# Moving operands shifted by spare bytes, so that each TensorE product reads at a chosen offset from its weights

## The chip, the cores and the metric

One NeuronCore of a Trainium2 chip runs the program. The metric is device time in microseconds (us), from the first to the last instruction of the program and what the runtime puts around it; lower is better.

## The reference

Two layers on a sequence of 256 tokens with 2048 features, in float32:

```python
h = x
h = h + conv_pool_mixer(rms_norm(h))   # w_in 2048x3072, 31-tap conv + layer norm, pools, w_out 2048x2048
h = h + swiglu(rms_norm(h))            # w_gate, w_up 2048x5632, w_down 5632x2048
h = h + short_conv_mixer(rms_norm(h))  # w_in 2048x6144, 3-tap conv, w_out 2048x2048
h = h + swiglu(rms_norm(h))
return rms_norm(h)
```

Nearly all the arithmetic is matrix products of the 256 tokens with weights, which are read once each from HBM (some 390 MB).

## The kernel before, in words

Activations lie with features on the 128 partitions and tokens along the free dimension. The weights come as 5904 blocks of 128x128, in the order in which they are used, in DMA units of at most 16 blocks (tile `w`). ScalarE rounds eight blocks at a time to float32r (`hi`, L114), VectorE or sometimes GpSimd subtracts to get the rest (`lo`, L121). Each `hi` and `lo` tile has 4096 bytes in a partition, a block 512.

An activation chunk of 128 features is split in the same way: its high half lies in the first 256 columns of a slice, its low half in the next 256 (2048 bytes together). These moving operands are four tiles: `xs` (16 slices, filled by each norm), `cat` (8 slices, the halves of the first mixer's output), `y` (22 slices, half of a SwiGLU's hidden layer) and `z` (16 slices, the short convolution's output).

For each block `product` issues one of two forms. The **wide** form, in both SwiGLUs and the second mixer, is one matmul of `hi` with all 512 columns (L163) and one of `lo` with the first 256 (L164): two weight loads and 768 columns. The **narrow** form, in the first mixer and for the last chunk of the last SwiGLU, is three matmuls of 256 columns (L166 and L167 with `hi`, L168 with `lo`): three weight loads and 768 columns.

All of a block's operands start at a multiple of 512 bytes from the start of their tiles, and the weight tiles have a multiple of 256. So within one stage the distance from the start of the weights to the start of the moving operand, modulo 256 bytes, is one number, which this document calls the **offset**. By the addresses in the built program it is 0 for `xs`, 32 for `cat`, and 96 for `y` and `z`.

A program-wide order of the instructions is set at build time; the pieces `hi` and `lo` are prepared four ahead of their use (LOOK), the DMAs one unit further. The first mixer's convolution runs on VectorE and ScalarE beside the products.

Of the kernel before, what the change touches and what calls it, by code (L numbers as in the profile page):

```python
# [12 lines left out]
F32R = mybir.dt.float32r  # L13
# [4 lines left out]
P = 128  # L18
T = 256
D = 2048  # L20
NC = D // P
DC = 1024
NA = DC // P
FF = 5632
NF = FF // P
NH = NF // 2
# [46 lines left out]
WARM = 9  # L73

KEEP = 8

POOL_SPLIT = range(96, 24 * NC + 16 + 7 * NC + 8)

# [6 lines left out]
def block_kernel(ctx: ExitStack, tc: tile.TileContext, xT: bass.AP, xtok: bass.AP, vec: bass.AP, wall: bass.AP, out: bass.AP):  # L85
    nc = tc.nc
    const = ctx.enter_context(tc.tile_pool(name="const", bufs=1))
    act = ctx.enter_context(tc.tile_pool(name="act", bufs=1))
# [35 lines left out]
    def next_block():  # L124
        b, i = cursor
        at = UNIT_AT[PIECES[i][0]] + PIECES[i][1]
        if b == at + PIECES[i][2]:
            ready.pop(i)
            i, at = i + 1, b
        for j in range(i, i + LOOK + 1):  # L130
            prepare(j)
        if i + LOOK < len(PIECES):
            for u in range(PIECES[i + LOOK][0] + 1, PIECES[i + LOOK][0] + AHEAD + 1):
                fetch(u)
        cursor[:] = [b + 1, i]
        hi, lo = ready[i]
        o = (b - at) * P
        return hi[:, o : o + P], lo[:, o : o + P]
# [8 lines left out]
    def tick():  # L147
        for name, q in queues.items():
            credit[name] = credit[name] + 1.0 if q else 0.0
            while q and credit[name] >= PACE[q[0][0]]:  # L150
                cost, step = q.popleft()
                credit[name] -= PACE[cost]
                step()

    def drain():
        while any(queues.values()):
            for q in queues.values():
                if q:
                    q.popleft()[1]()

    def product(acc, hi, lo, x, first, last, wide):
        if wide:
            nc.tensor.matmul(acc, hi, x, start=first, stop=False, skip_group_check=True)  # L163
            nc.tensor.matmul(acc[:, T:], lo, x[:, :T], start=False, stop=last, skip_group_check=True)  # L164
        else:
            nc.tensor.matmul(acc[:, :T], hi, x[:, :T], start=first, stop=False)  # L166
            nc.tensor.matmul(acc[:, :T], hi, x[:, T:], start=False, stop=False)  # L167
            nc.tensor.matmul(acc[:, :T], lo, x[:, :T], start=False, stop=last)  # L168

    def matmul_chunks(xs, ks, n=1, wide=False, behind=None):  # L170


        accs = [ps.tile([P, 2 * T], F32, name="acc") for _ in range(n)]
        for i, k in enumerate(ks):
            first, last = i == 0, i == len(ks) - 1
            for acc in accs:
                hi, lo = next_block()
                product(acc, hi, lo, xs[:, k, :], first, last, wide)
                tick()
            if behind is not None:  # L180
                behind(k)
        return accs
# [10 lines left out]
    def split(dst, src, scale=None):  # L193

        if scale is None:
            nc.scalar.copy(dst[:, :T], src)
            nc.vector.tensor_tensor(out=dst[:, T:], in0=src, in1=dst[:, :T], op=ALU.subtract)
        else:
            nc.scalar.activation(dst[:, :T], src, AF.Copy, scale=scale)
            nc.vector.scalar_tensor_tensor(out=dst[:, T:], in0=src, scalar=scale, in1=dst[:, :T], op0=ALU.mult, op1=ALU.subtract)  # L200
# [4 lines left out]
    def col(name, i):  # L205
        return v[:, VECS[name] + i : VECS[name] + i + 1]

    identity = v[:, VECS["identity"] :]
    h = act.tile([P, NC, T], F32, name="h")
    xs = act.tile([P, NC, 2 * T], F32R, name="xs")  # L210
    ones = const.tile([P, P], F32, name="ones")
    nc.gpsimd.memset(ones, 1.0)

# [14 lines left out]
    def rsqrt_of(*totals, scale, halves=False, st=None):  # L228
# [9 lines left out]
        if halves:  # L238

            idle = ps.tile([P, P], F32, name="idle", tag="acc")  # L240
            with tc.issue_after(mm.ins):
                for _ in range(KEEP):
                    nc.tensor.matmul(idle, ones, ones, start=True, stop=True)  # L243
# [27 lines left out]
    class Norm:  # L271


        def __init__(self, gain, final=False):
            self.gain, self.final = gain, final
            self.sums = []

        def add(self, c):
# [6 lines left out]

        def scale(self, c):
            if not self.final:
                split(xs[:, c, :], h[:, c, :], col(self.gain, c))

        def square(self, c):  # L290
            if c == 0:
# [16 lines left out]
    def project(src, ks, norm=None, wide=False, narrow_end=False):  # L308

        for n in range(NC):  # L310
            if narrow_end and n == NC - 1:
                wide = False
            (acc,) = matmul_chunks(src, ks, wide=wide)
            if wide:
                t = phase[0].tile([P, T], F32, name="cross", bufs=3)
                nc.scalar.copy(t, acc[:, T:])
                nc.vector.tensor_tensor(out=h[:, n, :], in0=h[:, n, :], in1=t, op=ALU.add)
            nc.vector.tensor_tensor(out=h[:, n, :], in0=acc[:, :T], in1=h[:, n, :], op=ALU.add)  # L318
            if norm is not None:
                norm.add(n)  # L320

    def scaled(acc, r, name, wide=False):
        if not wide:
            s = (phase[0] if name == "pv" else tmp).tile([P, T], F32, name=name, bufs=2)
            nc.vector.tensor_tensor(out=s, in0=acc[:, :T], in1=r, op=ALU.mult)
            return s
        s = summed(acc, name)
        nc.vector.tensor_tensor(out=s, in0=s, in1=r, op=ALU.mult)
        return s


    norm = Norm("mix_norm_e")
    nc.sync.dma_start(v[:, :NC], vec[:, :NC])

    def load(at, n):
# [30 lines left out]
    every = range(NC)  # L366
    with tc.tile_pool(name="m0", bufs=1) as m0, tc.tile_pool(name="ps_side", bufs=2, space=PSUM) as ps_side:
# [1 line left out]
        a_in = m0.tile([P, NA, pad + T], F32, name="a_in")  # L369
        nc.gpsimd.memset(a_in[:, :, :pad], 0.0)  # L370
        conv = m0.tile([P, NA, T], F32, name="conv")
        cat = m0.tile([P, NA, 2 * T], F32R, name="cat")
        total = m0.tile([P, 2, T], F32, name="total")

        sides, prods, state = {}, {}, {}
# [156 lines left out]

        project(xs, POOL_CHUNKS)
        drain()
        norm = Norm("ffn_norm0")
        project(cat, range(NA), norm)

    def swiglu(norm, following):
        with tc.tile_pool(name="ffn", bufs=1) as fp:
            phase[0] = fp  # L540
            y = fp.tile([P, NH, 2 * T], F32R, name="y")
            r = None
            for half in range(2):
                for f in range(NH):
                    (acc_g,) = matmul_chunks(xs, every, wide=True)
                    (acc_u,) = matmul_chunks(xs, every, wide=True)
                    if r is None:
                        r = norm.rstd()
                    gate = scaled(acc_g, r, "gate", True)
                    up = scaled(acc_u, r, "val", True)  # L550
                    nc.scalar.activation(gate, gate, AF.Silu)
                    nc.vector.tensor_tensor(out=up, in0=up, in1=gate, op=ALU.mult)
                    split(y[:, f, :], up)
                project(y, range(NH), following if half else None, wide=True, narrow_end=half and following.final)
# [1 line left out]
    x0.close()  # L556


    after = Norm("mix_norm_o")
    swiglu(norm, after)  # L560


    norm = Norm("ffn_norm1")
    with tc.tile_pool(name="m1", bufs=1) as m1:
        phase[0] = m1
        z = m1.tile([P, NC, 2 * T], F32R, name="z")
        pad = SW - 1
        r = None
        for c in range(NC):
            (acc_c,) = matmul_chunks(xs, every, wide=True)  # L570
            (acc_v,) = matmul_chunks(xs, every, wide=True)
            if r is None:
                r = after.rstd()
            cg = scaled(acc_c, r, "gate", True)
            vv = scaled(acc_v, r, "val", True)
            cv = m1.tile([P, pad + T], F32, name="cv", bufs=2)
            nc.gpsimd.memset(cv[:, :pad], 0.0)
            nc.vector.tensor_tensor(out=cv[:, pad:], in0=cg, in1=vv, op=ALU.mult)
            wc = VECS["conv_w_o"] + c * SW
            co = m1.tile([P, T], F32, name="co", bufs=2)  # L580
            nc.vector.tensor_scalar(out=co, in0=cv[:, :T], scalar1=v[:, wc : wc + 1], scalar2=None, op0=ALU.mult)
            for k in range(1, SW):
                nc.vector.scalar_tensor_tensor(out=co, in0=cv[:, k : k + T], scalar=v[:, wc + k : wc + k + 1], in1=co, op0=ALU.mult, op1=ALU.add)
            (acc_b,) = matmul_chunks(xs, every, wide=True)
            bg = scaled(acc_b, r, "pv", True)
            nc.vector.tensor_tensor(out=bg, in0=bg, in1=co, op=ALU.mult)
            split(z[:, c, :], bg)
        project(z, every, norm, wide=True)


    last = Norm("final_norm", final=True)
    swiglu(norm, last)
    halves = rsqrt_of(*last.sums, scale=1.0 / D, halves=True)
    with tc.tile_pool(name="fin", bufs=1) as fin:

# [90 lines left out]
```

## Time and profile before

| | |
|---|---|
| three runs | 2104.46, 2105.78, 2109.65 us; median 2105.78 |
| profiled execution | 2103.73 us, of which the span of the trace is 2102.0 |
| TensorE matmul busy | 2079.1 us (99%), 12584 records |
| weight loads busy | 1855.8 us (88%), beside the matmuls |
| VectorE, ScalarE, GpSimd busy | 66%, 50%, 10% |
| weights' DMA queue | 393.52 MB, 52.4% of 16 engines' time |
| TensorE's granted clock | 0.997 of full speed, mean |

A matmul's duration in the profile is from its start to its modelled end, and successive matmuls overlap; how fast they follow each other is read from the distance between their starts.

### The profile page before, as it was taken

What the parts mean: (1) busy time and instruction counts of PE and PEld (TensorE: products, weight loads), DVE (VectorE), ACT (ScalarE), POOL (GpSimd) and SP (SyncE); (2) the same over time, 40 slices, a digit from 0 to 9 for tenths busy, and PEclk for the clock granted to TensorE, in tenths of its full rate; (3) what the DMA queues carried; (4) which work ended last, traced back from release to release, by engine and by line L of the source; (5) the groups of instructions that cost most, each with busy time, mean ns of one, the idle gap of its engine ahead of it and who ended that gap; (6) DMA issues with size and microseconds to landing.
All of it is one profiled execution on the core that took longest, in us unless ns stands there. A gap on an engine that the chain in (4) does not pass through costs nothing.

```text
span 2102.0 us, 31608 instructions
## 1 busy us (share of the span) xinstructions
PE 2079.1 (99%) x12584; PEld 1855.8 (88%) x12584; DVE 1383.4 (66%) x1979; ACT 1060.9 (50%) x1571; POOL 200.6 (10%) x180
## 2 busy tenths in 40 slices
PE   8999999999999999999999999999999999999998
PEld 8999988888888888888888888888888888888887
DVE  6888866666556666666777777666666556666654
ACT  7776654444444444454444445554444444444453
POOL 3985200000000000011000001100000000000011
PEclk9999999999999999999999999999999999999999
DMA  8554455555555555555555555555555555555551
GB/s 326 187 191 168 158 184 197 183 198 182 194 185 188 193 187 194 183 196 182 183 198 182 198 183 193 180 189 198 183 196 184 189 192 183 198 182 199 182 192 68
DMA packets 56884, 395.53 MB, mean 188 GB/s; under 512 B 6432, under 2 KB 7200, under 8 KB 9760
## 3 DMA queue, kind: packets, MB, share of 16 engines
q1 hardware_dynamic: 56736, 393.52, 52.4%
q8 instruction: 98, 1.61, 0.3%
q14 instruction: 50, 0.41, 0.1%
HBM read 391.39 MB, written 2.10 MB: 187 GB/s over the span
## 4 chain that ended last, share of the span: by engine, by line
PE 98%; DMA 1%; DVE 1%; ACT 0%; SPq 0%; issue 0%; DVEq 0%; ACTq 0%
PE acc L163 57%; PE acc L164 30%; PE acc L166 4%; PE acc L168 4%; PE acc L167 4%; DMA rows<-in_xtok 0%; DMA h<-in_xT 0%; DVE res L603 0%; ACT hi L114 0%; PE st L237 0%; PE st L268 0%; DVE lo L121 0%; SPq L104 0%; ACT conv L475 0%; PE idle L243 0%
## 5 line engine op out<-in xcount | busy, mean ns | idle before, releaser
L114 ACT CAST hi<-w 128x1024 fp32r<-128x1024 f32 (+1 forms) x740 | 776.1, 1050 | 975.3 <-PE acc L163 621.0
L121 DVE TENSOR_TENSOR lo<-w,hi 128x1024 fp32r<-128x1024 f32 (+1 forms) x691 | 845.2, 1224 | 639.5 <-ACT hi L114 635.3
L163 PE MATMUL acc<-xs,hi 128*128 128x512 f32 x3584 | 1243.3, 391 | 0.0
L164 PE MATMUL acc<-xs,lo 128*128 128x256 f32 x3584 | 1004.7, 280 | 0.0
L163 PEld LDWEIGHTS acc<-xs,hi 128*128 128x128 f32 x3584 | 670.4, 187 | 146.2
L164 PEld LDWEIGHTS acc<-xs,lo 128*128 128x128 f32 x3584 | 678.1, 189 | 0.1
L163 PE MATMUL acc<-y,hi 128*128 128x512 f32 x1386 | 485.2, 393 | 0.0
L164 PE MATMUL acc<-y,lo 128*128 128x256 f32 x1386 | 386.4, 279 | 0.0
L163 PEld LDWEIGHTS acc<-y,hi 128*128 128x128 f32 x1386 | 259.4, 187 | 61.7
L164 PEld LDWEIGHTS acc<-y,lo 128*128 128x128 f32 x1386 | 259.9, 187 | 0.4
L298 POOL TENSOR_TENSOR sumsq<-sumsq,sq 128x256 f32<-128x256 f32 x56 | 58.8, 1050 | 1599.1 <-ACT sq L296 1599.1
L166 PE MATMUL acc<-xs,hi 128*128 128x256 f32 x512 | 144.0, 284 | 5.2 <-ACT hi L114 4.2
L167 PE MATMUL acc<-xs,hi 128*128 128x256 f32 x512 | 143.6, 283 | 0.0
L168 PE MATMUL acc<-xs,lo 128*128 128x256 f32 x512 | 141.3, 284 | 0.1
L121 POOL TENSOR_TENSOR lo<-w,hi 128x1024 fp32r<-128x1024 f32 x49 | 118.7, 2441 | 43.1 <-PE acc L167 34.3
L166 PEld LDWEIGHTS acc<-xs,hi 128*128 128x128 f32 x512 | 98.1, 192 | 6.2 <-ACT hi L114 5.0
L167 PEld LDWEIGHTS acc<-xs,hi 128*128 128x128 f32 x512 | 98.2, 192 | 0.0
L168 PEld LDWEIGHTS acc<-xs,lo 128*128 128x128 f32 x512 | 96.5, 192 | 0.5 <-DVE lo L121 0.5
L163 PE MATMUL acc<-z,hi 128*128 128x512 f32 x256 | 89.6, 393 | 0.0
L188 ACT COPY cross<-acc 128x256 f32<-128x256 f32 x224 | 80.6, 360 | 0.0
L164 PE MATMUL acc<-z,lo 128*128 128x256 f32 x256 | 71.3, 279 | 0.0
L318 DVE TENSOR_TENSOR h<-acc,h 128x256 f32<-128x256 f32 x112 | 47.2, 423 | 18.9 <-PE acc L168 13.2
(134 smaller groups left out, 1198.6 us busy)
## 6 DMA issues: line engine op xcount, KB each, us to landing
w<-in_wall SPq DMA_DIRECT2D x365, 1024.0 KB, 4.8
w<-in_wall SPq DMA_DIRECT2D x7, 512.0 KB, 7.7
rows<-in_xtok SPq DMA_DIRECT2D x2, 1024.0 KB, 7.9
h<-in_xT SPq DMA_DIRECT2D x7, 256.0 KB, 7.3
out<-res SPq DMA_DIRECT2D x2, 512.0 KB, 2.8
out<-res SPq DMA_DIRECT2D x2, 384.0 KB, 2.8
v<-in_vec SPq DMA_DIRECT2D x1, 260.0 KB, 6.7
h<-in_xT SPq DMA_DIRECT2D x2, 128.0 KB, 2.3
```

Of the source, the lines that this page charges most:

```text
L114: nc.scalar.copy(hi[:, : n * P], w)
L121: engine.tensor_tensor(out=lo[:, : n * P], in0=w, in1=hi[:, : n * P], op=ALU.subtract)
L163: nc.tensor.matmul(acc, hi, x, start=first, stop=False, skip_group_check=True)
L164: nc.tensor.matmul(acc[:, T:], lo, x[:, :T], start=False, stop=last, skip_group_check=True)
L166: nc.tensor.matmul(acc[:, :T], hi, x[:, :T], start=first, stop=False)
L167: nc.tensor.matmul(acc[:, :T], hi, x[:, T:], start=False, stop=False)
L168: nc.tensor.matmul(acc[:, :T], lo, x[:, :T], start=False, stop=last)
L188: nc.scalar.copy(t, acc[:, T:])
L298: nc.gpsimd.tensor_tensor(out=self.sums[0], in0=self.sums[0], in1=sq, op=ALU.add)
L318: nc.vector.tensor_tensor(out=h[:, n, :], in0=acc[:, :T], in1=h[:, n, :], op=ALU.add)
```

## The change

Each moving tile gets some spare bytes (`xs` 256, the others 128), and the operands become views that start some bytes into the tile. `xs` is now used at two places: 32 bytes in for the first mixer, 160 bytes in for the other three norms. `y` and `z` start 64 bytes in. `cat` starts where it did. Who reads and writes what, the number of instructions and their order on every engine stay as they are.

```diff
+XS_M0 = 32
+XS_F0 = 160
+XS_M1 = 160
+XS_F1 = 160
+Y_F0 = 64
+Y_F1 = 64
+Z_M1 = 64
+CAT = 0
...
-    xs = act.tile([P, NC, 2 * T], F32R, name="xs")
+    xs_room = act.tile([P, NC * 2 * T + 64], F32R, name="xs")
+    def moving(room, at, n):
+        return room[:, at // 4 : at // 4 + n * 2 * T].rearrange("p (c t) -> p c t", c=n)
...
-        def __init__(self, gain, final=False):
+        def __init__(self, gain, at=0, final=False):
             self.gain, self.final = gain, final
+            self.xs = moving(xs_room, at, NC)
...
-                split(xs[:, c, :], h[:, c, :], col(self.gain, c))
+                split(self.xs[:, c, :], h[:, c, :], col(self.gain, c))
...
-        cat = m0.tile([P, NA, 2 * T], F32R, name="cat")
+        cat = moving(m0.tile([P, NA * 2 * T + 32], F32R, name="cat"), CAT, NA)
...
-            y = fp.tile([P, NH, 2 * T], F32R, name="y")
+            y = moving(fp.tile([P, NH * 2 * T + 32], F32R, name="y"), at, NH)
...
-                    (acc_g,) = matmul_chunks(xs, every, wide=True)
-                    (acc_u,) = matmul_chunks(xs, every, wide=True)
+                    (acc_g,) = matmul_chunks(norm.xs, every, wide=True)
+                    (acc_u,) = matmul_chunks(norm.xs, every, wide=True)
...
-        z = m1.tile([P, NC, 2 * T], F32R, name="z")
+        z = moving(m1.tile([P, NC * 2 * T + 32], F32R, name="z"), Z_M1, NC)
```

The weight tiles move up by 256 bytes, which leaves the offsets as the numbers say:

| products | blocks | offset before | offset now |
|---|---|---|---|
| wide, `xs` | 3584 | 0 | 160 |
| wide, `y` and `z` | 1386 + 256 | 96 | 160 |
| narrow, `xs` | 512 | 0 | 32 |
| narrow, `cat` | 144 | 32 | 32 |
| narrow, `y` (last chunk) | 22 | 96 | 160 |

## Rows read from the trace of the kernel before

**Rows 1.** The page: the span, busy time by engine, and the slices' granted clock.

```profile
span 2102.0 us, 31608 instructions
...
PE 2079.1 (99%) x12584; PEld 1855.8 (88%) x12584; DVE 1383.4 (66%) x1979; ACT 1060.9 (50%) x1571; POOL 200.6 (10%) x180
...
PEclk9999999999999999999999999999999999999999
```

**Rows 2.** What TensorE's instructions waited for: us in total, times, longest.

```profile
PE acc L166 <- ACT hi L114: 4.2, 3, 1.7
PE acc L166 <- ACT cat L477: 3.4, 1, 3.4
PE st L268 <- DVE diag L260: 2.8, 1, 2.8
```

**Rows 3.** By stage: us, busy us (records) of each engine, clock, DMA.

```profile
core 0: us, PE busy (x) PEld busy (x) DVE busy (x) ACT busy (x) POOL busy (x), PEclk, DMA share, GB/s
0.00:47.00 47.00, 40.77 (x310) 39.25 (x311) 27.95 (x52) 34.30 (x53) 10.61 (x40) 1.00 0.89 342
47.00:260.00 213.00, 205.82 (x1703) 204.64 (x1702) 183.04 (x324) 153.98 (x266) 142.27 (x83) 0.98 0.50 178
260.00:505.00 245.00, 245.00 (x1417) 216.23 (x1417) 158.69 (x227) 120.49 (x179) 0.00 (x0) 1.00 0.53 188
```

**Rows 4.** Wide hi matmuls in stretches of xs, y, z: count, durations, first and last start.

```profile
L163 PE MATMUL acc<-xs,hi x616: 390/391/392, 290.6 to 503.8; 128*128 128x512 f32 x154
L163 PE MATMUL acc<-y,hi x321: 392/394/395, 515.8 to 627.8; 128*128 128x512 f32 x161
L163 PE MATMUL acc<-z,hi x224: 392/393/394, 1273.9 to 1352.0; 128*128 128x512 f32 x112
```

**Rows 5.** The same for narrow first matmuls: xs twice, cat, y.

```profile
L166 PE MATMUL acc<-xs,hi x136: 283/283/284, 55.0 to 103.6; 128*128 128x256 f32 x136
...
L166 PE MATMUL acc<-xs,hi x87: 283/283/284, 165.0 to 196.0; 128*128 128x256 f32 x87
...
L166 PE MATMUL acc<-cat,hi x93: 277/280/281, 226.9 to 259.1; 128*128 128x256 f32 x93
...
L166 PE MATMUL acc<-y,hi x22: 279/282/285, 2080.9 to 2088.5; 128*128 128x256 f32 x22
```

**Rows 6.** Timeline of a wide stretch: start us, duration us.

```profile
300.01 0.39 PE L163 MATMUL acc<-xs,hi 128*128 128x512 f32 x1
300.24 0.28 PE L164 MATMUL acc<-xs,lo 128*128 128x256 f32 x1
300.35 0.39 PE L163 MATMUL acc<-xs,hi 128*128 128x512 f32 x1
```

**Rows 7.** Counts of the products by moving tile, whole span, and of the start.

```profile
L163 PE MATMUL acc<-xs,hi 128*128 128x512 f32 x3584 | 1243.3, 391 | 0.0
...
L163 PE MATMUL acc<-y,hi 128*128 128x512 f32 x1386 | 485.2, 393 | 0.0
...
L163 PE MATMUL acc<-z,hi 128*128 128x512 f32 x256 | 89.6, 393 | 0.0
...
L166 PE MATMUL acc<-cat,hi x144: 277/280/583, 150.4 to 259.1; 128*128 128x256 f32 x144
...
L166 PE MATMUL acc<-xs,hi x97: 278/283/385, 4.7 to 46.8; 128*128 128x256 f32 x97
```

**Rows 8.** Preparation of weights: busy us, mean ns of one, idle before.

```profile
L121 DVE TENSOR_TENSOR lo<-w,hi 128x1024 fp32r<-128x1024 f32 x688 | 843.6, 1227 | 637.0 <-ACT hi L114 632.8 <-PE acc L164 3.6
L114 ACT CAST hi<-w 128x1024 fp32r<-128x1024 f32 x737 | 774.7, 1052 | 972.8 <-PE acc L163 621.0 <-issue 295.8 <-PE acc L167 42.1
```

More of the change, by code (lines that the diff above doesn't have):

```diff
@@ L329, in scaled @@
         return s
-    norm = Norm("mix_norm_e")
+    norm = Norm("mix_norm_e", XS_M0)
+    xs = norm.xs
     nc.sync.dma_start(v[:, :NC], vec[:, :NC])
@@ L534, in block_kernel, with swiglu @@
         drain()
-        norm = Norm("ffn_norm0")
+        norm = Norm("ffn_norm0", XS_F0)
         project(cat, range(NA), norm)
-    def swiglu(norm, following):
+    def swiglu(norm, following, at):
         with tc.tile_pool(name="ffn", bufs=1) as fp:
             phase[0] = fp
-            y = fp.tile([P, NH, 2 * T], F32R, name="y")
+            y = moving(fp.tile([P, NH * 2 * T + 32], F32R, name="y"), at, NH)
             r = None
@@ L556, in block_kernel @@
     x0.close()
-    after = Norm("mix_norm_o")
-    swiglu(norm, after)
-    norm = Norm("ffn_norm1")
+    after = Norm("mix_norm_o", XS_M1)
+    swiglu(norm, after, Y_F0)
+    norm = Norm("ffn_norm1", XS_F1)
     with tc.tile_pool(name="m1", bufs=1) as m1:
         phase[0] = m1
-        z = m1.tile([P, NC, 2 * T], F32R, name="z")
+        z = moving(m1.tile([P, NC * 2 * T + 32], F32R, name="z"), Z_M1, NC)
         pad = SW - 1
@@ L569, in block_kernel @@
         for c in range(NC):
-            (acc_c,) = matmul_chunks(xs, every, wide=True)
-            (acc_v,) = matmul_chunks(xs, every, wide=True)
+            (acc_c,) = matmul_chunks(after.xs, every, wide=True)
+            (acc_v,) = matmul_chunks(after.xs, every, wide=True)
             if r is None:
@@ L583, in block_kernel @@
                 nc.vector.scalar_tensor_tensor(out=co, in0=cv[:, k : k + T], scalar=v[:, wc + k : wc + k + 1], in1=co, op0=ALU.mult, op1=ALU.add)
-            (acc_b,) = matmul_chunks(xs, every, wide=True)
+            (acc_b,) = matmul_chunks(after.xs, every, wide=True)
             bg = scaled(acc_b, r, "pv", True)
@@ L591, in block_kernel @@
     last = Norm("final_norm", final=True)
-    swiglu(norm, last)
+    swiglu(norm, last, Y_F1)
     halves = rsqrt_of(*last.sums, scale=1.0 / D, halves=True)
```

## The prediction

> **What bounds the kernel now.** The page comes first: TensorE's matmuls are busy for 2079.1 of 2102.0 us, at the full granted clock in every slice [rows 1], which is the 2.4 GHz level. The list of waits comes next, since a busy share alone doesn't say that TensorE never waits: its longest entries are 4.2, 3.4 and 2.8 us, all in the first mixer or at a norm [rows 2], and the wide stretch from 260 to 505 us is 245.00 us busy out of 245.00 [rows 3]. The weights' supply is not what it runs against: DMA moves 188 GB/s there and moved 342 in the first stage [rows 3]; per eight blocks ScalarE's cast takes 1052 ns and VectorE's subtraction 1227 [rows 8], while eight wide blocks take TensorE 2.8 us. So the time is the number of blocks times the time in which TensorE gets through one, and this change touches only that.
>
> How long a block takes is read from starts, first to last in an undisturbed stretch, divided by the count less one.
>
> - Wide, `xs`, offset 0: 290.6 to 503.8 us over 615 steps [rows 4], 346.7 ns.
> - Wide, `y`, offset 96: 515.8 to 627.8 over 320 steps, 350.0 ns; `z`, also 96: 1273.9 to 1352.0 over 223, 350.2 ns [rows 4]. I take 350.1 for both.
> - Narrow, `xs`, offset 0: 55.0 to 103.6 over 135 steps, 360 ns [rows 5].
> - Narrow, `cat`, offset 32: 226.9 to 259.1 over 92 steps, 350 ns [rows 5].
> - Narrow, `y`, offset 96: 2080.9 to 2088.5 over 21 steps, 362 ns, known to 5 ns only [rows 5].
>
> The reader is to see that the same number of columns, 768, takes four different times, and that the time goes with the offset. It could go with something else that differs between stages, but the nearest neighbours speak against that: the projection of `xs` at 165 to 196 us has the same code, the same form and the same busy VectorE beside it as that of `cat`, and its 86 steps take 31.0 us, 360 ns [rows 5], against 350.
>
> 768 columns at 2.4 GHz are 320 ns. What is left over is 26.7 ns (wide, 0), 30.1 (wide, 96), 40 (narrow, 0) and 30 (narrow, 32). A wide block has two weight loads, a narrow one three. Per load that is **13.3 ns at offset 0 in both forms**, 15.05 at 96 in the wide form, about 14 at 96 in the narrow form, and **10.0 at 32** in the narrow form. That both forms agree at offset 0 is the best sign that the excess belongs to a load that runs beside a streaming operand, not to the number of columns. In the timeline the hi matmul takes 230 ns to the next start and the lo matmul 110 to 120 [rows 6], so both of a wide block's matmuls carry some of it.
>
> Check of the sum: 3584 x 346.7 + 1642 x 350.1 + 534 x 360 + 144 x 350 ns, with the counts of [rows 7], is 1242.6 + 574.9 + 192.2 + 50.4 = 2060 us. The other 42 us of the span are the start, the tail and the norms, which the change leaves alone.
>
> **The change, part by part.** No instruction is added, removed or moved; only addresses differ. The spare bytes cost nothing in time, since no instruction writes them.
>
> *Narrow `xs`, 0 to 32.* The row of `cat` gives the price directly: 360 to 350 ns, 10 ns for each of 512 blocks, 5.1 us. Of these, 97 lie in the first 47 us [rows 7], where the loads move 342 GB/s and DMA is 0.89 busy [rows 3], so that TensorE waits for data and their 1.0 us is likely hidden. The other 415 are worth 4.2 us, in a stage where VectorE is busy 183 of 213 us and TensorE idles 7.2 us [rows 3]. Part of what TensorE gains there it will wait for the convolution's chain. I take half, **2.1 us**, with bounds of 0 and 5.1.
>
> *Wide `xs`, 0 to 160, and wide `y` and `z`, 96 to 160.* No row shows 160. The rows give three levels per load: 10.0, 13.3 and 15.05 ns. The one good offset of before, 32, lies exactly 128 bytes from 160, and the worse ones, 0 and 96, lie on either side of it. If what collides repeats every 128 bytes, 160 is the good place; nothing in the trace contradicts that, and nothing proves it. At 10.0 per load a wide block takes 320 + 20 = 340.0 ns. That is 6.67 x 3584 = **23.9 us** for `xs` and 10.1 x 1642 = **16.6 us** for `y` and `z`. As bounds I go beyond the rows by the distance between their best and worst level, 5.05 ns per load: 4.95 per load gives 329.9 ns a block, 60.2 + 33.2 = 93.4 us gained; 20.1 per load gives 360.2 ns, 48.4 + 16.6 = 65.0 us lost. I take 10.0, since the narrow form showed it at the offset to which 160 stands nearest under a halved period.
>
> *Narrow `y`, 96 to 160*, is 22 blocks: even 10 ns on each is 0.2 us, left out.
>
> *Would something else become late?* At 340 ns a unit of 16 blocks (1 MB) is wanted every 5.4 us, 193 GB/s, far from the 342 that the first stage reached; VectorE's share in a wide stage goes from 158.7 of 245 to the same work in 240 us [rows 3]. So the cover of the preparation holds.
>
> **Sum.** 23.9 + 16.6 + 2.1 = 42.6 us. The profiled execution took 2103.73 us (span 2102.0 and 1.7 around it), so it would take 2061.1. The median of the runs shown is 2.05 us above the profiled execution, which makes **2063 us**, 2.0% faster.
>
> The Trainium skill says the opposite in two places. "TensorE: Matmul & The Clock Gate", in its part on what happens when you issue a matmul, gives TensorE two independent read ports, so that loading the next weights takes nothing from the running matmul; "SBUF — State Buffer", under who interferes with whom, has only the port pair that VectorE and GpSimd share cause contention. By these rules the offset is worth nothing, and the sum would be zero: 2105.8 us. Here the trace does not agree with them, by the 350 against 360 ns above.
>
> **The rivals.**
>
> *160 is like 0.* The wide blocks get 13.3 ns per load: `xs` stays at 346.7, `y` and `z` gain 3.4 x 1642 = 5.6 us, with 2.1 of the narrow form 7.7 us: 2098. For it: 13.3 is the commonest level in the rows, at two offsets and in both forms. Against it: only that 160 isn't 0.
>
> *160 is like 96: slower.* 96 and 160 differ by 64 bytes, and both lie 32 past a multiple of 64. If the collision goes with the place within 64 bytes, `xs` goes from 346.7 to 350.1: 3.4 x 3584 = 12.2 us lost, nothing changes for `y` and `z`, 2.1 us are gained: 2116. Speaking against it: in the narrow form 32 and 96 also lie 64 apart, and their blocks differ, 350 against about 362. It decides for slower from 2.4 ns a block upwards (8.4 us on `xs`, less 2.1, is 6.3 us). Beyond it lies a level that no row shows: 360.2 ns a block ends at 2105.8 + 65.0 - 2.1 = 2169.
>
> *The offset does nothing*, as the pages above would have it, and the stages differ for another reason, such as what a matmul's accumulators or the engines beside it do. Then 2105.8. The two `xs` stretches at 360 with different work around them [rows 5] speak against it.
>
> *The gain is larger than the row of `cat` says*: towards 329.9 ns, 2105.8 - 93.4 - 2.1 = 2010. Speaking for it is only that no row shows the floor.
>
> **How the numbers follow.** The level of 10 ns per load, within a step of 1.7 ns either way (half of 3.3; 336.6 to 343.4 ns a block, which is 2046 to 2081): 0.52. Better still: 0.08. Like 0: 0.14. Like 96: 0.13. Worse than every row: 0.08. No effect: 0.05. A measurement of this kernel tells 0.3% (6.3 us) from no change. Like 0 is 7.7 us faster with the narrow gain and 5.6 without, so I split it, 0.09 faster and 0.05 same. Faster is then 0.52 + 0.08 + 0.09 = 0.69, same 0.05 + 0.05 = 0.10, slower 0.13 + 0.08 = 0.21. The range reaches from halfway into the better case, 2028, over the rivals at 2098, 2106 and 2116, and leaves out the worst case and half of the better one: 0.12. As the signs are mixed, the likeliest case's own range is 2046 to 2081.
>
> **What would show it.** Right: the starts of L163 on `xs`, `y` and `z` follow each other at one and the same distance, near 340 ns, and the first mixer's L166 at 350 on `xs`. The first of these proves the levels per load; `y` and `xs` at different times would prove that the offset isn't what counts. Wrong: 346.7 or 350.1 in all wide stages (the rivals), or wide stages with waits on `hi` or `lo` that weren't there. A first mixer that ends as late as before, with `xs` at 350 ns, would show the narrow gain hidden.

## The result, and the profile after

The changed kernel takes 2094.9 us (median of 4 runs, 2093.66 to 2095.70) against 2106.03 before (4 runs, 2104.46 to 2109.65). The ratio is 0.9948, with a 95% interval of 0.9936 to 0.9960: 0.5% faster. Forecast were 2063 us, with 2028 to 2117 as the range. The direction was right, the gain a quarter of what was said. Of the 26 runs of the kernel before in the first table of experiments below, one took 3290.17 us at a granted clock of 0.587 and is out of the ratios there.

The page of the kernel after answers [rows 1]. TensorE's longest waits are those of [rows 2], and its busy time is less by 8.9 us, the span by 8.8.

```profile
PE acc L176 <- ACT hi L124: 4.2, 3, 2.4
PE acc L176 <- ACT cat L494: 3.4, 1, 3.4
PE st L283 <- DVE diag L275: 2.8, 1, 2.8
```

```profile
span 2093.2 us, 31608 instructions
...
PE 2070.2 (99%) x12584; PEld 1850.5 (88%) x12584; DVE 1383.1 (66%) x1979; ACT 1061.8 (51%) x1571; POOL 200.5 (10%) x180
...
PEclk9999999999999999999999999999999999999999
```

The wide hi matmul (now L173) in stretches of `xs`, `y` and `z` answers [rows 4]; columns as there, the last two times are the first and the last start.

```profile
L173 PE MATMUL acc<-xs,hi x613: 391/391/392, 287.7 to 499.8; 128*128 128x512 f32 x154
...
L173 PE MATMUL acc<-y,hi x290: 391/392/392, 522.7 to 622.9; 128*128 128x512 f32 x145
...
L173 PE MATMUL acc<-z,hi x188: 391/392/392, 1279.8 to 1344.7; 128*128 128x512 f32 x188
```

`xs` takes 212.1 us for 612 steps, 346.6 ns a block; `y` 100.2 for 289, 346.7; `z` 64.9 for 187, 347.1. All wide stages run at the 346.7 ns that `xs` had before. Offset 160 brings `y` and `z` from 350.1 to 346.7, not to the forecast 340.0, and does nothing for `xs`.

The narrow first matmuls (L176) of `xs` and `cat` answer [rows 5].

```profile
L176 PE MATMUL acc<-xs,hi x141: 277/280/281, 54.0 to 103.0; 128*128 128x256 f32 x141
...
L176 PE MATMUL acc<-xs,hi x73: 277/278/281, 167.8 to 193.0; 128*128 128x256 f32 x73
...
L176 PE MATMUL acc<-cat,hi x89: 277/278/280, 225.0 to 255.8; 128*128 128x256 f32 x89
```

49.0 us over 140 steps and 25.2 over 72 are 350 ns: `xs` in the first mixer now goes as fast as `cat` did and does. How much of that reaches the end of the stage is seen where the first wide products start, after the change and before it:

```profile
L173 PE MATMUL acc<-xs,hi x16: 391/392/397, 256.5 to 261.7; 128*128 128x512 f32 x16
```

```profile
L163 PE MATMUL acc<-xs,hi x8: 391/391/399, 259.5 to 261.9; 128*128 128x512 f32 x8
```

3.0 us. With 1642 x 3.4 ns = 5.6 us for `y` and `z` that is 8.6 of the 8.8 us by which these two spans differ, so the whole gain is found in these two traces. The 3.0 is of this pair alone, since the start of the program differs from one execution to the next: in the five traces with narrow `xs` at 32 (after, after_again, narrow_only, all_0, all_32) the first wide product starts between 255.2 and 258.5 us, in the five with it at 0 (before, both_32, yz_only, xs_only, yz_32) between 259.5 and 262.1.

### The profile page after: what moved, and what is told of

Its sections match the earlier page's. It is cut to its first block, busy times and chain, and to the rows that moved or that the text cites. A ratio compares the mean times of both kernels' runs of the same rounds, so it can differ in the third digit from the quotient of the medians.

```text
span 2093.2 us, 31608 instructions
## 1 busy us (share of the span) xinstructions
PE 2070.2 (99%) x12584; PEld 1850.5 (88%) x12584; DVE 1383.1 (66%) x1979; ACT 1061.8 (51%) x1571; POOL 200.5 (10%) x180
## 4 chain that ended last, share of the span: by engine, by line
PE 98%; DMA 1%; DVE 1%; ACT 0%; SPq 0%; issue 0%; DVEq 0%; ACTq 0%
PE acc L173 57%; PE acc L174 29%; PE acc L176 4%; PE acc L178 4%; PE acc L177 3%; DMA rows<-in_xtok 0%; DMA h<-in_xT 0%; DVE res L620 0%; ACT hi L124 0%; PE st L252 0%; DVE lo L131 0%; PE st L283 0%; SPq L114 0%; ACT conv L492 0%; PE idle L258 0%
## 5 line engine op out<-in xcount | busy, mean ns | idle before, releaser
L173 PE MATMUL acc<-xs,hi 128*128 128x512 f32 x3584 | 1243.2, 392 | 0.0
L173 PEld LDWEIGHTS acc<-xs,hi 128*128 128x128 f32 x3584 | 672.7, 188 | 148.5
L173 PE MATMUL acc<-y,hi 128*128 128x512 f32 x1386 | 480.4, 392 | 0.0
L173 PEld LDWEIGHTS acc<-y,hi 128*128 128x128 f32 x1386 | 259.9, 188 | 57.2
L176 PE MATMUL acc<-xs,hi 128*128 128x256 f32 x512 | 142.7, 282 | 5.2 <-ACT hi L124 4.2
L176 PEld LDWEIGHTS acc<-xs,hi 128*128 128x128 f32 x512 | 96.9, 190 | 6.1 <-ACT hi L124 4.8
L173 PE MATMUL acc<-z,hi 128*128 128x512 f32 x256 | 88.7, 392 | 0.0
```

## The experiments

All edits are against the changed kernel. The theories that stood against each other: **A**, the price per weight load is set by the offset in the same way in both forms, and 160 is merely no good place; **B**, 160 is as good a place as 32, but the wide form gains nothing from a good place, because 346.7 is its floor; **C**, offsets repeat after 64 or 128 bytes.

**sweep_a: another offset in each stage.**

```diff
-XS_M0 = 32
-XS_F0 = 160
-XS_M1 = 160
-XS_F1 = 160
-Y_F0 = 64
-Y_F1 = 64
-Z_M1 = 64
-CAT = 0
+XS_M0 = 160
+XS_F0 = 32
+XS_M1 = 64
+XS_F1 = 128
+Y_F0 = 96
+Y_F1 = 128
+Z_M1 = 192
+CAT = 32
...
```

The tiles get spare bytes to match, here and in the runs below.

> Each stage has another offset, so one profile gives a curve: wide xs at 32 (first SwiGLU), 64 (second mixer), 128 (second SwiGLU), wide y at 192 and 224, wide z at 32; narrow xs at 160, cat at 64. Theory A (the place is wrong: the excess per weight load is set by the offset modulo 256 in the same way in both forms, and 160 is simply no good offset): wide at 32 takes 340.0 ns a block (10.0 per load), and narrow at 160 takes 360. Theory B (the form is wrong: 160 is as good an offset as 32, and the wide form gains nothing from a good offset): wide at 32 takes 346.7, as at 160, and narrow at 160 takes 350. Theory C (offsets repeat after 64 or 128 bytes): wide at 32 and 160 alike, 64 and 192 alike, 0 and 128 alike. Where A holds for some offset, the wide stages have a block under 343.

2116.55 us, one run beside one of the kernel before at 2105.76. Stretches of the wide stages, `xs` at 32, `y` at 192, `xs` at 64 and 128, `y` at 224, `z` at 32, as offsets:

```profile
L173 PE MATMUL acc<-xs,hi x607: 390/390/390, 289.8 to 499.9; 128*128 128x512 f32 x152
...
L173 PE MATMUL acc<-y,hi x284: 397/397/398, 524.9 to 624.9; 128*128 128x512 f32 x142
...
L173 PE MATMUL acc<-xs,hi x626: 392/397/398, 1028.9 to 1249.7; 128*128 128x512 f32 x157
...
L173 PE MATMUL acc<-xs,hi x596: 387/396/398, 1390.8 to 1599.7; 128*128 128x512 f32 x199
...
L173 PE MATMUL acc<-y,hi x290: 392/397/402, 1627.8 to 1729.9; 128*128 128x512 f32 x145
...
L173 PE MATMUL acc<-z,hi x177: 390/390/390, 1290.7 to 1351.7; 128*128 128x512 f32 x177
```

Per block these are 346.7 at 32 (`xs` and `z`), 353.4 at 192, 353.3 at 64, 351.1 at 128 and 353.3 at 224 ns. The narrow form gives, in the first stretch and then in the projection at 160, and for `cat` at 64:

```profile
L176 PE MATMUL acc<-xs,hi x139: 277/281/283, 53.8 to 102.9; 128*128 128x256 f32 x139
...
L176 PE MATMUL acc<-xs,hi x75: 277/280/282, 167.8 to 193.9; 128*128 128x256 f32 x75
...
L176 PE MATMUL acc<-cat,hi x80: 279/279/279, 226.9 to 254.8; 128*128 128x256 f32 x80
```

355.8, 352.7 and 353.2 ns. Theory A falls on the wide form at 32: the best place of the narrow form gives 346.7 there, not 340.0. Of B half holds: the wide form does no better at 32 than at 160, but the narrow form at 160 takes 355.8 and 352.7, not the 350 of a place as good as 32. C falls as well, though some pairs do look alike (32 and 160, 64 and 192): 0 and 128 differ, 346.7 and 351.1, and in the narrow form 32 and 160 differ, 350 and 353 to 356. What is left is B's floor, with a curve of times above it that each form has for itself.

**sweep_b: finer offsets, and tiles exchanged.** `xs` at 16, 48 and 96 in the three wide norms, `y` at 0 and 80, `z` at 8, both narrow tiles at 128, by the same constants.

> Finer offsets, and tiles exchanged: wide xs at 16, 48 and 96, y at 0 and 80, z at 8; narrow xs and cat at 128. If the offset alone decides, xs at 96 takes 350.1 ns a block and y at 0 takes 346.7, the times that the other tile had there before. If the tile or the stage decides (what other engines do beside it), xs stays at 346.7 and y at 350.1. If the step of the effect is 32 bytes or more, 16 and 8 take what 0 takes, 346.7, and 48 what 32 takes.

2109.25 us, one run. `xs` at 16 and at 96, `y` at 0, `z` at 8, by stretch:

```profile
L173 PE MATMUL acc<-xs,hi x604: 387/387/388, 290.7 to 499.7; 128*128 128x512 f32 x151
...
L173 PE MATMUL acc<-xs,hi x613: 392/392/394, 1385.7 to 1599.9; 128*128 128x512 f32 x154
...
L173 PE MATMUL acc<-y,hi x284: 392/394/395, 526.7 to 624.9; 128*128 128x512 f32 x142
...
L173 PE MATMUL acc<-z,hi x192: 400/400/400, 1285.7 to 1353.2; 128*128 128x512 f32 x192
```

346.6 (16), 350.0 (96), 347.0 (`y` at 0) and 353.4 ns (8). Tiles exchanged, times exchanged: the offset decides here, not the tile or the stage. That `z` at 8 took longer than 0 and 16 did says that the effect is finer than 32 bytes, which was not the expectation; each of these offsets was seen in one or two stages, and the runs on patterns below show that one offset can hold more than one time. `y` at 80 took 349.8, `xs` at 48 351.2, narrow at 128 355.8.

**both_32: the same offsets at other addresses.**

```diff
-        hi = whl.tile([P, PIECE * P], F32R, name="hi")
-        lo = whl.tile([P, PIECE * P], F32R, name="lo")
+        hi = whl.tile([P, PIECE * P + 64], F32R, name="hi")[:, 8 : 8 + PIECE * P]
+        lo = whl.tile([P, PIECE * P + 64], F32R, name="lo")[:, 8 : 8 + PIECE * P]
...
```

with `xs`, `y`, `z` and `cat` 32 bytes into their tiles.

> Weights and moving operands both start 32 bytes later, so that every offset is that of the kernel before, at other addresses. If the distance between them decides: 346.7 (wide xs), 350.1 (y, z), 360 (narrow xs), 350 (cat), and the whole at 2106 us. If the absolute place of the moving operand decides (32 past a multiple of 64), wide xs takes 350.1 as y did, or narrow xs 350 as cat did, and the whole moves by 5 to 12 us.

2105.40 us, one run. `xs` wide 210.1 us over 606 steps, 346.7; `y` 99.7 over 285, 349.8; narrow `xs` 48.9 over 136, 360; `cat` 26.6 over 76, 350. All four as before: for this shift of 32 bytes the distance counts, not the address. One stretch differed: the start of the first SwiGLU went at 353 ns a block (19 steps from 273.35 to 280.06 us) until two other matmuls came between, behind which, from 281 us on, it took 346.7. That led to the runs on patterns below.

**loads: fewer and more weight loads.** `part` names what a stage does: the first SwiGLU leaves out the lo matmul, the second mixer splits the hi matmul in four, and the second SwiGLU does the lo matmul twice. Offsets are those of before.

```diff
...
-        if wide:
+        if wide and part[0] == "hi":
+            nc.tensor.matmul(acc, hi, x, start=first, stop=last, skip_group_check=True)
+        elif wide and part[0] == "hi lo lo":
+            nc.tensor.matmul(acc, hi, x, start=first, stop=False, skip_group_check=True)
+            for j in range(2):
+                nc.tensor.matmul(acc[:, T:], lo, x[:, :T], start=False, stop=last and j == 1, skip_group_check=True)
+        elif wide and part[0] == "quarters":
+            for j in range(4):
+                nc.tensor.matmul(acc[:, j * P : (j + 1) * P], hi, x[:, j * P : (j + 1) * P], start=first and j == 0, stop=False, skip_group_check=True)
+            nc.tensor.matmul(acc[:, T:], lo, x[:, :T], start=False, stop=last, skip_group_check=True)
+        elif wide:
...
```

> Offsets of before (0 for xs, 96 for y), and work left out or added in the wide stages: the first SwiGLU leaves out the lo matmul (one load, 512 columns), the second mixer splits the hi matmul into four of 128 columns (five loads, 768 columns), the second SwiGLU does the lo matmul twice (three loads, 1024 columns). The results are not the reference's. If the excess goes by weight loads (13.3 ns each at 0): 226.7 ns for the block of hi alone, 386.7 for the five loads, 466.7 for the three. If it goes by columns and matmuls (one column in 16 and 3.3 ns a matmul, which fits 230 and 116.7): 230.0, 356.7 and 463.3. If a load has a least time of its own near the 113 to 120 ns of the narrow matmuls, the quarters take that long each, and the five-load block some 560 to 600.

2273.04 us, one run of other work, so its stretches alone are read. Hi alone on `xs` at 0 and on `y` at 96 (L173), hi lo lo on both (L175 is its hi matmul), and the last matmul of the quarters (L181):

```profile
L173 PE MATMUL acc<-xs,hi x586: 389/389/389, 289.8 to 422.4; 128*128 128x512 f32 x196
...
L173 PE MATMUL acc<-y,hi x313: 392/394/399, 431.7 to 504.5; 128*128 128x512 f32 x157
...
L175 PE MATMUL acc<-xs,hi x643: 390/395/395, 1299.9 to 1599.5; 128*128 128x512 f32 x161
...
L175 PE MATMUL acc<-y,hi x319: 393/394/398, 1614.6 to 1764.6; 128*128 128x512 f32 x160
...
L181 PE MATMUL acc<-xs,lo x742: 330/332/334, 759.9 to 1179.4; 128*128 128x256 f32 x186
```

At offset 0 one load beside 512 columns takes 226.7 ns a block and three loads beside 1024 columns 466.7: 213.3 + 13.3 and 426.7 + 3 x 13.3, on the nanosecond. The theory of columns and matmuls (230.0, 463.3) falls. At 96 it is 233.3 and 471.7, which is 20 and 15 per load, so there the surcharge depends on how the matmuls follow each other. In every form each matmul has one load of its own, so a price per matmul, whatever its columns, would fit 226.7, 346.7 and 466.7 as well; no run here tells the two apart. The quarters take 566 ns, 113 for each of five loads, as the third possibility had it: in the trace of that stretch one load starts 108 to 124 ns behind the other.

**narrow_only, yz_only, xs_only: the three parts of the change, each alone.**

```diff
-XS_F0 = 160
-XS_M1 = 160
-XS_F1 = 160
-Y_F0 = 64
-Y_F1 = 64
-Z_M1 = 64
+XS_F0 = 0
+XS_M1 = 0
+XS_F1 = 0
+Y_F0 = 0
+Y_F1 = 0
+Z_M1 = 0
```

is narrow_only; yz_only keeps the last three at 64 and sets `XS_M0` to 0; xs_only keeps the first three at 160 and sets `XS_M0` to 0.

> Only the first mixer's xs moves (0 to 32); the wide products keep the offsets of before. If the parts add up and the first mixer gives what the trace of the changed kernel shows (its first wide product starts 2.9 us earlier): 2.9 us faster, 2103. If the narrow form's whole 10 ns a block arrives at the end: 5.1 us, 2101. If the first mixer waits for VectorE instead: no change.

> Only y and z move (96 to 160). 1642 blocks by 3.4 ns: 5.6 us faster, 2100.4, whatever the theory, if wide time goes by offset alone. If the changed kernel's gain came through xs, no change.

> Only the wide products' xs moves (0 to 160). If 160 and 0 are the same floor of the wide form, as 16, 32 and 160 all showed 346.7 ns: no change, 2106. If the prediction's 340 ns were hidden elsewhere in the changed kernel: 24 us faster, 2082.

| kernel | median us (runs) | ratio to before, 95% interval |
|---|---|---|
| before | 2105.26 (26) | |
| narrow_only | 2100.52 (11) | 0.9975, 0.9966 to 0.9984 |
| yz_only | 2109.89 (10) | 1.0022, 1.0013 to 1.0031 |
| xs_only | 2104.54 (11) | 0.9997, 0.9987 to 1.0006 |

narrow_only came out at the upper expectation: nearly all of the narrow form's 5.1 us arrive. xs_only does nothing, as the floor has it. yz_only was **slower** where 5.6 us were expected to be gained, whatever the theory. Its trace shows where: `y` at 160, and `xs` at 0 in the first half of the first SwiGLU and in its second half, behind `y`.

```profile
L173 PE MATMUL acc<-y,hi x288: 391/392/392, 529.7 to 629.2; 128*128 128x512 f32 x144
...
L173 PE MATMUL acc<-xs,hi x607: 391/391/391, 294.7 to 504.7; 128*128 128x512 f32 x152
...
L173 PE MATMUL acc<-xs,hi x661: 395/398/403, 644.8 to 878.0; 128*128 128x512 f32 x166
```

`y` does its part: 99.5 us over 287 steps, 346.7. But `xs` at one and the same offset runs at 346.5 in the one half (210.0 over 606) and at 353.3 in the other (233.2 over 660). Both SwiGLUs do it: 2 x 704 x 6.6 ns = 9.3 us lost, less 5.6 gained, is the 3.7 us to which the measured 4.6 answers. So at offset 0 the stream has more than one steady time. That the place at which it enters picks one was the idea that the runs with all_0 below tested.

**lo_at_0: hi and lo weights at different offsets.**

```diff
...
+STAGE_ENDS = np.cumsum([656, 704, 352, 704, 352, 768, 256, 704, 352, 704]).tolist()
+LO_SHIFT = (64, 32, 64, 96, 128, 160, 192, 224, 16, 48, 80)
...
-        lo = whl.tile([P, PIECE * P], F32R, name="lo")
+        at = LO_SHIFT[sum(UNIT_AT[u] + o >= e for e in STAGE_ENDS)] // 4
+        lo = whl.tile([P, PIECE * P + 64], F32R, name="lo")[:, at : at + PIECE * P]
```

with all wide moving operands at 0.

> The hi weights stay at offset 0 in every wide stage, the lo tiles' views start 32, 64, 96, 128, 160, 192, 224, 16, 48 and 80 bytes later, one value a stage in the order of the program (first mixer 64). Theory D (a matmul collides with the weights that are loaded beside it, which are those of the next matmul): the hi matmul's time changes with the lo tile's place, the lo matmul's stays, and some pairing may leave a block below 346.7. Theory E (13.3 ns a load is a fixed price of a load beside a stream at full clock, collisions come on top): no stage is below 346.7, some are above, up to some 353.

2107.10 us, one run. Shifts of 32, 160, 192, 224 and 48:

```profile
L177 PE MATMUL acc<-xs,hi x614: 389/394/398, 289.8 to 502.3; 128*128 128x512 f32 x154
...
L177 PE MATMUL acc<-xs,hi x656: 393/396/397, 1029.8 to 1259.8; 128*128 128x512 f32 x164
...
L177 PE MATMUL acc<-z,hi x174: 396/396/396, 1289.7 to 1349.7; 128*128 128x512 f32 x174
...
L177 PE MATMUL acc<-xs,hi x606: 392/395/398, 1389.8 to 1603.5; 128*128 128x512 f32 x152
...
L177 PE MATMUL acc<-xs,hi x650: 392/392/392, 1744.6 to 1969.6; 128*128 128x512 f32 x163
```

346.7, 351.1, 346.8, 353.2 and 346.7 ns; 64, 16 and 80 also gave 346.7, 128 346.9 and 96 351.5. No pairing goes below 346.7, as theory E expected. In the `z` stage the hi matmul lasts 396 ns where [rows 4] had 391 for `xs`, and yet the block is as short. By the starts, the hi matmul takes 233.3 and the lo matmul 113.3 ns there, against 230.0 and 116.7 for `xs` before: time moves between the two, and their sum stays.

**all_32, all_0, yz_32, after_again: which offsets hold one pattern.** all_32 has 32 everywhere (`XS_F0 = XS_M1 = XS_F1 = 32`, `Y_F0 = Y_F1 = Z_M1 = 192`); all_0 has 0 in all wide stages and 32 in the narrow ones; yz_32 has `xs` at 0 throughout and `y` and `z` at 32; after_again is the changed kernel.

> Wide and narrow products all at offset 32. If 346.7 is the wide form's floor and 32 reaches it as 160 does: every wide stage at 346.7 and the first mixer at 350, the same time as the changed kernel, 2095. If 32 and 160 differ in a way that only whole runs show: over 6 us apart.

> Narrow products at 32, all wide ones at 0, so that no wide stage follows one of another offset. If offset 0 has two steady patterns (346.7 and 353.3 ns) and the faster one is kept where nothing shifts the stream: 2095, as the changed kernel. If any stage of offset 0 falls into the slower one, as xs did behind y at 160: 4.7 us more for each such stage of 704 blocks, 2100 to 2109.

> xs at 0, y and z at 32. If what comes ahead picks the pattern of xs at offset 0 by the place at which the stream is when it starts: xs behind y is at 346.7 or at 353.3 in both SwiGLUs alike, and the stages that start behind a norm, where TensorE waits, need not be as those behind y. If 353.3 was an accident of those runs: 346.7 everywhere, about 2100.

> The changed kernel on the same chip as the two above: 2095, 0.5% below the kernel before, every wide stage at 346.7 and the first mixer at 350.

| kernel | median us (runs) | ratio to before, 95% interval |
|---|---|---|
| before | 2105.93 (15) | |
| all_32 | 2095.12 (5) | 0.9948, 0.9935 to 0.9960 |
| all_0 | 2104.44 (11) | 0.9994, 0.9985 to 1.0003 |
| after_again | 2096.04 (5) | 0.9952, 0.9938 to 0.9965 |
| yz_32 | 2100.57 (1) | beside 2105.93 |

32 and 160 serve alike, so neither kernel beats the other. Their wide stages all run at 346.7, but the first mixer is not at 350 throughout, as both expectations had it: its projection of `xs` took 353 in both profiles. all_0 gives the gain of the changed kernel away again. Its trace has, all at offset 0, `xs` and `y` of the first SwiGLU's first half, `y` of its second half, and `xs` of the second SwiGLU's first half:

```profile
L173 PE MATMUL acc<-xs,hi x613: 391/391/391, 289.8 to 501.9; 128*128 128x512 f32 x154
...
L173 PE MATMUL acc<-y,hi x287: 392/395/395, 524.8 to 624.0; 128*128 128x512 f32 x144
...
L173 PE MATMUL acc<-y,hi x294: 395/398/403, 888.7 to 992.2; 128*128 128x512 f32 x147
...
L173 PE MATMUL acc<-xs,hi x615: 395/398/403, 1381.7 to 1598.6; 128*128 128x512 f32 x154
```

346.6, 346.9, 353.2 and 353.3 ns. No change of offset lies ahead of the third and fourth, so the idea that the faster pattern is kept where nothing shifts the stream is wrong: something else on the way moves it too, and which wait or start does it was not tried. What picks the time at offset 0 stays open. With the last stage of `y` (86.6 us over 245 steps, 353.5) these are at least 294, 615 and 246 blocks by 6.6 ns, 7.6 of the 9.3 us by which all_0 lies above all_32. In yz_32 `xs` behind `y` took 228.4 us over 659 steps, 346.6: entered from 32, offset 0 kept the faster pattern, and no wide stage was slower.

## Why the prediction was wrong

The bottleneck was read rightly: TensorE streams without a wait in the wide stages, time is blocks times time per block, and the time per block goes with the offset (both_32, sweep_b), though at 0 it can take either of two values within one program (yz_only, all_0). The excess of 13.3 ns at offset 0 for each matmul with its load was read rightly too (loads); that it belongs to the load and not to the matmul is not shown. Nothing else became late.

| term | predicted us | measured us |
|---|---|---|
| wide `xs`, 0 to 160 | 23.9 | 0 (xs_only, 0.9987 to 1.0006) |
| wide `y`, `z`, 96 to 160 | 16.6 | 5.6 (trace after) |
| narrow `xs`, 0 to 32 | 2.1, 0 to 5.1 | 3.0 (trace after), 4.7 (narrow_only) |
| sum | 42.6 | 8.8 (spans), 11.1 (medians) |

The step that failed is "I take 10.0, since the narrow form showed it at the offset to which 160 stands nearest under a halved period". It carried a level from one form into the other and from one place to another, and both halves fail. The wide form at 32 itself, the place where the narrow form has its 10.0 ns per load, has 13.3 (sweep_a, all_32): the level isn't to be had. And a period of 128 bytes doesn't hold: 0 and 128 differ in the wide form, 346.7 and 351.1 ns a block (sweep_a), and in the narrow form itself 160 takes 355.8 or 352.7 where 32 takes 350. That both forms agreed at 13.3 at offset 0 was taken as a sign that they share the whole curve; they share one point. The trace of before could have warned: the commonest level in its rows, at which the rival "160 is like 0" was set, was also the lowest that the wide form showed. That rival said 2098 and was right in mechanism; its narrow term, 2.1, was too small against the 4.7 of narrow_only, since the waits that were to take half of it did not come: TensorE idles 7.2 us in the first mixer as before (202.79 busy of 210 us from 47 to 257, against 205.82 of 213 in [rows 3]).

What the Trainium skill says in "TensorE: Matmul & The Clock Gate" (what happens when you issue a matmul: two independent read ports, so loading weights takes nothing from a running matmul) and in "SBUF — State Buffer" (who interferes with whom: only the port pair that VectorE and GpSimd share causes contention) was weighed as the rule by which nothing changes. The runs do not agree with it: `xs` takes 346.7 ns at 32 and 353.3 at 64 (sweep_a). Where the two operands meet is not shown by that.

What stays open is why 13.3 ns remain for every matmul with its load in the wide form at each of the offsets and pairings tried, and why the narrow form can go to 10.0. The 113 ns per load of the quarters shows only that narrow matmuls, at 350 / 3 = 116.7 ns, lie close to the pitch of the loads.

## What to carry to other kernels

Where TensorE streams without waits, divide a stretch between first and last start by its steps and compare stages: a few nanoseconds per block that follow no difference in work point to where the operands lie against each other. Prefer offsets at which all stages held one time (here 32 or 160 for wide products) to one that is as fast only at times (here 0); for narrow products 32 was the best one tried, at 350 or 353 ns. Set them for every tile at once: the change of `y` and `z` alone cost 4.6 us. A level seen in one form of instruction is a forecast for that form alone; one profile with another offset in each stage gives a first curve, in which an offset with two steady times shows only one of them.

## What was not expected of the hardware

One offset can hold two steady times for hundreds of blocks. Wide products at 0 run at 346.7 or 353.3 ns a block, narrow ones at 32 at 350 or 353, until something disturbs the stream. The program doesn't fix which: the changed kernel's projection of `xs`, at 350 in the first profile, took 25.8 us over 73 steps, 353 ns, in that of after_again.

```profile
L176 PE MATMUL acc<-xs,hi x74: 278/278/278, 168.0 to 193.8; 128*128 128x256 f32 x74
```

And in the one stretch looked at, the excess is gone at the lower clock. From 203.0 to 209.9 us, at the first mixer's tail, TensorE has nothing but two small matmuls to do, and then restarts at the lower granted clock; the changed kernel's stretch of that (columns as in [rows 3]) and its matmuls' starts are

```profile
210.00:212.00 2.00, 2.00 (x10) 2.00 (x11) 0.57 (x1) 2.00 (x5) 0.00 (x0) 0.50 0.00 0
```

```profile
211.14 0.41 PE L177 MATMUL acc<-cat,hi 128*128 128x256 f32 x1
211.35 0.41 PE L178 MATMUL acc<-cat,lo 128*128 128x256 f32 x1
211.57 0.41 PE L176 MATMUL acc<-cat,hi 128*128 128x256 f32 x1
211.78 0.41 PE L177 MATMUL acc<-cat,hi 128*128 128x256 f32 x1
211.99 0.41 PE L178 MATMUL acc<-cat,lo 128*128 128x256 f32 x1
```

At a granted clock of 0.50, the 1.2 GHz level, four steps take 0.85 us, 213 ns each: 256 columns at 1.2 GHz and nothing on top, where the same matmuls at full clock have 10 ns of excess on 106.7.
